# A build-time planner's order from backward schedules, repeated and replayed

## The chip, the cores and the metric

The kernel runs on one core of one Trainium2 chip. The metric is the device time in microseconds (us) of one execution. Times before are of three runs; the profile is of one more execution.

## The reference

One inference step of a one-layer hybrid decoder. A prompt of 2048 tokens and 8 decode sequences of 8 tokens go through the same layer:

```python
h = rmsnorm(x, norm_w)
z = h @ w_in                       # 1024 x 3600
q, k, v, qb, kb, vb, g_lr, gate_a, gate_b = split(z)
q, k = rope(rmsnorm(q)), rope(rmsnorm(k))
o_a = attend(q, k, v)              # 8 heads x 64; windows (128,1), (512,4), (2048,16), mixed by their softmax denominators
log_a = log_sigmoid(g_lr @ w_gate_up + b_gate) / 16
o_b, s_fin = gla_chunked(qb / 8, kb, vb, log_a, s0)   # 4 heads, key 64, value 128
o_b = rmsnorm(o_b, gla_norm_w)
mixed = concat(o_a * silu(gate_a), o_b * silu(gate_b))
y = x + mixed @ w_out
```

The decode tokens attend to caches of 2048 keys and values for each sequence and update a recurrent state. Outputs are `y` of both parts, the new keys and values, and the GLA states. All is float32 outside; the kernel splits float32 operands of the large products into two fp16 parts.

## The kernel before

The program is written as one long trace of instructions for five engines: PE (matmul), DVE, ACT, POOL and SP, which issues all the DMAs on its queue. It is tiled by 128 tokens, 16 tiles for the prompt.

Its stages, in the order of the code:

- Input projections (`project`, matmuls at L1614 into `acc_q`, `acc_k`, `acc_v`, `acc_qkb`, `acc_g`, `acc_vb`, `acc_gb`), each with its own block of weights, `load_w` at L1144 and L1145. Three weight blocks fit at a time. `post` evacuates them, to scratch tensors in DRAM (`vb_d`, `gw_d`, `ga_d` and others).
- Prompt attention (`attend`): scores `s` on PE (L894), mask and minimum on DVE (L902, which also writes to `o`), the exponential `p` on ACT (L905), transposes `t` on PE (L912), a split `pt` into fp16 halves on ACT, DVE or POOL (L874 to L879), products `O` on PE (L927).
- Decode-side dot products (`dot`, 128 of them): a product `pr` on POOL (L1469) and its sum `sck` on DVE (L1470). They share a region of SBUF with other things that the GLA stage opens later.
- GLA (`gla_core`, `gla_prompt`): small fp32 matmuls (`sc_e` at L730, `U` L1777, `O` L1785 and L1791), in a chain over 16 chunks through a state `Sbd`; `gla_out` scales the output (`ob_c`, L785) and stores it in `ob_d`. The gate-b projection `acc_gb` is woven with it.
- Output: `combine` loads three attention branches (`oc`), the GLA output and gates (`obl`, `gwl`, `gal`) and mixes them (`tc`, `mix`); the result is split into fp16 (`mt`), transposed (`tm`, L1950), copied (`mh`), and multiplied with the output weights (`Y`, L1985). Its buffers take the room of the GLA stage's buffers. `inv_o`, which every evacuation of `Y` needs, needs all of the gate-b projection.
- Decode attention (`sample_pair`), beside the output stage: value blocks of 1 MB (`sv_b`, L2265, 24 of them) and fp32 matmuls `OS` (L2234).

The order in which each engine runs its instructions isn't that of the code. At the end of the trace the class `Plan` reads all the instructions, works out which depends on which (`dep`) or must stay behind which (`behind`), prices each (`price`: `busy`, how long its engine is taken; `late`, when its result is there; `lands` for a DMA's landing), and runs a list scheduler over the whole program (`order`). That scheduler simulates the five engines and the DMA queue forwards in time; where an engine has several ready instructions it takes the one with the lowest `prio`. PE's true fp32 matmuls (`slow`) have a queue of their own, and `bias` makes it stay with the kind it is at. `fix` then writes the found order into the program as dependencies without semaphores, and the framework emits each engine's queue in that order.

Before, the priority came from one pass of `rank`: an instruction's longest path to the end of the program, with no regard to engines being taken by other work:

```python
plan = Plan(tc, nc)
far = plan.rank()
plan.fix(plan.order([-f for f in far], 2000.0)[1])
```

Of the kernel before, what the change touches and what calls it, by code (L numbers as in the profile page):

```python
# [7 lines left out]
F32 = mybir.dt.float32  # L8
# [43 lines left out]
class Plan:  # L52
# [3 lines left out]
    def __init__(self, tc, nc, cross=35.0, traffic=1.15, lanes=8, room=212832):  # L56

        self.tc, self.cross, self.traffic = tc, cross, traffic
        self.lanes, self.room = lanes, room
        traced = nc.cur_bb.bb.instructions  # L60
        self.at = {i.name: n for n, i in enumerate(traced)}
        self.ins = [
            i for i in traced
            if type(i).__name__ not in ("BassTilePoolBoundary", "InstTileManualSchedule")
        ]
        self.eng = [str(i.engine).split(".")[-1] for i in self.ins]
        self.bits, self.pools = {}, {p.id: p for p in tc.info.pools}
        self.read()
        self.depend()
        self.price()  # L70
# [192 lines left out]
    def price(self):  # L263
# [22 lines left out]
            return r * (2 if a.dtype in (F16, BF16) else 4)  # L286

        self.busy, self.late, self.lock = [], [], []
        self.slow, self.columns, self.lands = set(), {}, {}
        for i, e in zip(self.ins, self.eng):  # L290
            ts, os_ = tensors(i.ins), tensors(i.outs)
            kind = type(i).__name__
# [4 lines left out]
            elif e == "PE":  # L297
                n = cells(os_[0])
                size, place = tuple(i.tile_size)[1], tuple(i.tile_position or (0, 0))[1]
                wide = [x for x in range(4) if size == P or place <= 32 * x < place + size]  # L300
# [7 lines left out]
                else:  # L308
                    n *= 2 if step >= 4 else 1
                    busy, late = max(n / 2.4 + 2.4, 55.5), 165 + n / 2.4  # L310
                self.columns[len(self.busy)] = wide
                busy *= 1.03
                late = max(busy, late)
            elif e == "SP":
# [105 lines left out]

    def order(self, prio, bias=0.0):

        from heapq import heappop, heappush

        N = len(self.dep)
        left = [len(d) + len(b) for d, b in zip(self.dep, self.behind)]
        ready, start, done = [0.0] * N, [0.0] * N, [0.0] * N
        soon = {e: [] for e in self.ENGINES}
        now = {e: [] for e in self.ENGINES}
        wide = []  # L430
        free = {e: 0.0 for e in self.ENGINES}
        held = {"DVE": 0.0, "Pool": 0.0}
        column, last, mode, queue = [0.0] * 4, 0.0, False, 0.0
        out = {e: [] for e in self.ENGINES}
# [36 lines left out]
        def arrive(e, t):  # L471
            while soon[e] and soon[e][0][0] <= t:
                _, pr, n = heappop(soon[e])
                heappush(wide if e == "PE" and n in self.slow else now[e], (pr, n))

        for n in range(N):
            if not self.dep[n] and not self.behind[n]:
                released(n)
        for _ in range(self.real):
            best = None  # L480
            if len(out["SP"]) >= self.lanes:
                free["SP"] = max(free["SP"], done[out["SP"][-self.lanes]] + self.cross + 20)
# [12 lines left out]
            line = now[e]  # L495
            if e == "PE" and wide:
                if not line or wide[0][0] <= line[0][0] + (bias if mode else -bias):
                    line = wide
            _, n = heappop(line)
            out[e].append(n)  # L500
            start[n] = t
            if e == "SP":
                free[e] = t + self.busy[n]
                queue = max(queue, free[e]) + self.late[n]
                done[n] = queue + self.lands[n]
            elif e == "PE":
                at = self.columns[n]
                s = max(t, last + 6, max(column[c] for c in at))
                if (n in self.slow) != mode:
                    s, mode = max(s, max(column) + 93), not mode  # L510
                last = start[n] = s
                for c in at:
                    column[c] = s + self.busy[n]
                free[e] = max(s, min(column)) if len(at) < 4 else s + self.busy[n]
                done[n] = s + self.late[n] + (100 if mode else 0)
# [11 lines left out]
        return max(done), out  # L527

    def fix(self, out):

# [11 lines left out]
def tile_hymba(ctx: ExitStack, tc: tile.TileContext, A: dict):  # L542
# [1752 lines left out]
        weave(out, [sample_attention(), 4 * 9])  # L2295

    plan = Plan(tc, nc)
    far = plan.rank()
    plan.fix(plan.order([-f for f in far], 2000.0)[1])


# [92 lines left out]
```

## Time and profile before

| | |
|---|---|
| median of 3 runs | 1388.49 us (1387.33 to 1389.8) |
| the profiled execution's own time | 1387.66 us |
| its span, first to last instruction | 1385.1 us |
| mean granted TensorE clock | 0.97 |
| PE busy | 1244.2 us (90%) |
| DVE busy | 1008.1 us (73%) |
| ACT busy | 844.7 us (61%) |
| POOL busy | 639.5 us (46%) |
| DMA | 283.25 MB, 205 GB/s over the span |

Busy time is the time in which an engine had at least one instruction under way. PE's matmuls are pipelined, so a busy PE is not PE at its peak, and weight loads (PEld) run beside them. The granted clock is the share of full speed that TensorE's throttle gave; it is either 1 or 0.5 at a moment in this trace. The rest of the time lies in waits, which the prediction shows by stretch.

### The profile page before, as it was taken

How to read it: one execution, taken by the hardware profiler on the slowest of the kernel's cores; microseconds unless marked ns; L12 is line 12 of the kernel's file. 1: busy time of each engine (PE TensorE's matmuls, PEld its weight loads, DVE VectorE, ACT ScalarE, POOL GpSimd, SP SyncE). 2: the span in 40 equal slices, each digit the busy share in tenths (PEclk: the TensorE clock that was granted, in tenths of full speed). 3: DMA queues.
4: the chain of work that ended last, by engine and by line, in shares of the span. 5: the costliest groups of instructions: out<-in, count | busy, mean ns of one | idle time of the engine just before them, and what ended most of it. 6: DMA issues, size and time to landing. Idle time of an engine off the chain costs nothing.

```text
span 1385.1 us, 26375 instructions
## 1 busy us (share of the span) xinstructions
PE 1244.2 (90%) x8942; PEld 739.4 (53%) x8942; DVE 1008.1 (73%) x2459; ACT 844.7 (61%) x2259; POOL 639.5 (46%) x564
## 2 busy tenths in 40 slices
PE   5999988987889789998899999999989839999998
PEld 2444455555456556655667656665555415445443
DVE  6897787888889978767665338778889775566632
ACT  6465588786678869776778347787768541222220
POOL 0155447787677555543212546645574332233310
PEclk9999999998999999999999999999999969999999
DMA  8579747968986797899765534325334389999822
GB/s 298 179 194 268 206 132 202 226 199 213 207 288 178 170 308 242 248 249 280 187 181 154 144 102 110 109 84 179 103 100 145 104 309 344 343 380 345 323 79 70
DMA packets 236121, 283.25 MB, mean 205 GB/s; under 512 B 116353, under 2 KB 147154, under 8 KB 232914
## 3 DMA queue, kind: packets, MB, share of 16 engines
q1 hardware_dynamic: 235986, 281.57, 67.9%
q8 instruction: 70, 1.15, 0.4%
q14 instruction: 65, 0.53, 0.1%
HBM read 183.19 MB, written 75.24 MB: 187 GB/s over the span
## 4 chain that ended last, share of the span: by engine, by line
PE 36%; DVE 8%; ACT 7%; DMA 6%; issue 3%; POOL 1%; SPq 1%; DVEq 0%; ACTq 0%; POOLq 0%
PE Y L1985 10%; PE acc_vb L1614 4%; PE acc_g L1614 4%; PE acc_gb L1614 4%; DMA qb<-q_d 2%; PE OS L2234 1%; PE sc_e L730 1%; ACT p L905 1%; PE t L912 1%; PE O L1791 1%; PE acc_qkb L1614 1%; DMA o_d<-o 1%; DVE qbd L706 1%; PE O L1785 1%; PE O L927 1%
## 5 line engine op out<-in xcount | busy, mean ns | idle before, releaser
L1614 PEld LDWEIGHTS <-hr 128*128 128x128 f16 x1824 | 175.1, 99 | 125.0 <-issue 29.7
L1469 POOL TENSOR_TENSOR pr<-k,qb 128x512 f32<-128x512 f32 x128 | 176.9, 1382 | 133.4 <-DVE sck L1470 62.7
L905 ACT ACTIVATE p<-p,o 128x256 f32<-128x256 f32 (+1 forms) x384 | 172.7, 453 | 53.5 <-DVE o L902 43.7
L1614 PEld LDWEIGHTS <-hl 128*128 128x128 f16 x1248 | 119.7, 98 | 128.2 <-issue 18.7
L1985 PE MATMUL Y<-w_o,mh 128*128 128x512 f16 x768 | 181.1, 381 | 3.6 <-DVE xr L1992 1.7
L927 PE MATMUL O<-v,pt 128*128 128x128 f16 x1200 | 145.9, 224 | 8.6 <-POOL pt L879 3.5
L879 POOL TENSOR_TENSOR pt<-p,pt 128x512 f16<-128x512 f32 (+1 forms) x80 | 93.0, 1163 | 125.6 <-ACT pt L878 94.7
L912 PE MATMUL t<-ident,p 128*128 128x128 f32 x600 | 132.2, 294 | 16.3 <-ACT p L905 10.4
L1614 PE MATMUL acc_g<-w_g,hr 128*128 128x272 f16 (+1 forms) x768 | 130.6, 276 | 3.3 <-ACT vbs L1263 2.0
L1614 PE MATMUL acc_vb<-w_vb,hr 128*128 128x512 f16 x384 | 122.1, 384 | 1.6 <-DVE so_g L1163 1.5
L927 PEld LDWEIGHTS <-pt 128*128 128x128 f16 x1200 | 100.2, 101 | 43.3 <-POOL pt L879 7.2
L1470 DVE TENSOR_REDUCE sck<-pr 128x8 f32<-128x512 f32 x128 | 87.3, 682 | 48.9 <-POOL pr L1469 48.2
L1614 PE MATMUL acc_v<-w_v,hl 128*128 128x512 f16 x384 | 120.2, 384 | 2.0 <-DMA hl<-ht 1.0
L1614 PE MATMUL acc_k<-w_k,hl 128*128 128x512 f16 x384 | 114.8, 379 | 4.5 <-DVE vp L1276 2.9
L1614 PE MATMUL acc_q<-w_q,hl 128*128 128x512 f16 x384 | 116.2, 379 | 2.8 <-ACT zs_q L1189 2.4
L1985 PEld LDWEIGHTS <-mh 128*128 128x128 f16 x768 | 71.2, 98 | 84.5 <-issue 7.5
L894 PE MATMUL s<-kk,qq 128*128 128x256 f16 (+1 forms) x512 | 84.8, 270 | 29.4 <-DVE o L902 21.7
L912 PEld LDWEIGHTS t<-ident,p 128*128 128x128 f32 x600 | 79.3, 147 | 50.1 <-ACT p L905 28.0
L1614 PE MATMUL acc_gb<-w_gb,hr 128*128 128x512 f16 x384 | 95.7, 399 | 7.8 <-DVE so_gb L1163 7.8
L902 DVE CUSTOM_DVE_ANT_0 p<-s,m3w,scl_s 128x128 f32<-128x128 f32 (+1 forms) x256 | 87.8, 396 | 19.8 <-DMA o_d<-o 8.9
L2033 POOL TENSOR_TENSOR tc<-oc,w 128x512 f32<-128x512 f32 x32 | 42.8, 1354 | 118.7 <-DVE w L2025 67.9
L1614 PE MATMUL acc_qkb<-w_qkb,hr 128*128 128x512 f16 x288 | 85.1, 379 | 0.0
(534 smaller groups left out, 2723.1 us busy)
## 6 DMA issues: line engine op xcount, KB each, us to landing
k<-in_cache_k_win SPq DMA_DIRECT2D x104, 256.0 KB
sv_b<-in_cache_v_win SPq DMA_DIRECT2D x24, 1024.0 KB
hr<-h_d SPq DMA_DIRECT2D x44, 512.0 KB
qb<-q_d SPq DMA_DIRECT2D x64, 256.0 KB
oc<-o_d SPq DMA_DIRECT2D x48, 264.0 KB
o_d<-o SPq DMA_DIRECT2D x64, 132.0 KB
x<-in_x_prompt SPq DMA_DIRECT2D x16, 512.0 KB
h_d<-hl SPq DMA_DIRECT2D x16, 512.0 KB
```

The source lines that it names most:

```text
L706: DVE.tensor_tensor(qbd[:, :, :n].rearrange("p i (m B) -> p i m B", B=B), qv[:, :, 1, :].unsqueeze(1).to_broadcast([P, 2, M, B]), ev[:, 1: ...
L879: POOL.tensor_tensor(l, f, h, ALU.subtract)
L894: PE.matmul(s_ps[:, i * w : (i + 1) * w], q, k, start=(n == 0), stop=(n == len(prods) - 1),)
L902: DVE.tensor_tensor_reduce(s[:, sl], s_ps[:, sl], mask, neg, BIG, ALU.add, ALU.min, nmf(i))
L905: ACT.activation(s[:, sl], s[:, sl], AF.Exp, bias=nmf(i), scale=-1.0, accum_out=denf(i))
L912: PE.transpose(p_ps[:, i * P : (i + 1) * P], t["s"][:, i * P : (i + 1) * P], ident[:])
L927: PE.matmul(o_, t["pt"][:, c, (i * nb + b) * P : (i * nb + b + 1) * P], vf(i, b), start=(n == 0), stop=(n == 2 * nb - 1),)
L1469: POOL.tensor_tensor(pr[:], kt, qt, ALU.mult)
L1470: DVE.tensor_reduce(out, pr[:].rearrange("p (u k d) -> p u k d", u=2, k=4), AX.X, ALU.add)
L1614: PE.matmul(z, a_[:, k, :], w[:, p_, k, cols], start=(k == 0 and i == 0), stop=(k == KT - 1 and i == 2),)
L1985: PE.matmul(Y[:], a_[:, k, :], w_[:, part, k, :512], start=(i == 0), stop=(i == len(prods) - 1),)
L2033: eng.tensor_tensor(t_[:], oc[:, g, :, 0:64], w[:, g].unsqueeze(2).to_broadcast([P, NH, HD]), ALU.mult,)
```

## The change

No operation of the computation changes; what changes is the order in which the planner puts them.

- `settle` replaces the single pass. It runs eight rounds of: schedule forwards with `order`, then backwards from the end with `backward`, and take the places of the backward schedule as the next round's priorities. The first round uses `rank` as before.
- While it plans, it uses other prices: every DMA lands 500 ns later, SP's transfers take 1.1 times as long, a hand-over between engines costs 50 ns in place of 35. The bias is 1000 in place of 2000.
- Each round's order is replayed (`replay`, the engines' order held) in four disturbed versions of the true prices (`other`: DMA times drawn at random, a quarter of the other instructions 30 ns longer). The order with the lowest sum of the four ends is kept.
- `order` has a model of the TensorE clock: array work (`area`) in a window of 3413 ns. Where it was under 0.4 of the window, PE's instructions of the next window cost twice as much. And PE holds on to fp32 matmuls by the bias only while the recent array work is over half a window (`keep`); else fp32 must be ahead of fp16 by the bias.

```diff
+        self.window, self.least = 3413.0, 0.5
...
+                four = 4 if len(self.busy) in self.slow else 2 if ts[0].dtype == F32 else 1
+                rows = -(-list(ts[0].ap)[0][1] // 32) / 4
+                self.area[len(self.busy)] = four * cells(os_[0]) / 2.4 * rows * len(wide) / 4
...
             if e == "PE" and wide:
-                if not line or wide[0][0] <= line[0][0] + (bias if mode else -bias):
+                while recent and recent[0][0] < t - self.window:
+                    active -= recent.popleft()[1]
+                keep = mode and active > self.least * self.window
+                if not line or wide[0][0] <= line[0][0] + (bias if keep else -bias):
                     line = wide
...
+                if int(s // self.window) > turn:
+                    half = work < 0.4 * self.window or int(s // self.window) > turn + 1
+                    turn, work = int(s // self.window), 0.0
+                work += self.area[n]
+                active += self.area[n]
+                recent.append((s, self.area[n]))
+                own = self.busy[n] * (2 if half else 1)
                 for c in at:
-                    column[c] = s + self.busy[n]
+                    column[c] = s + own
...
+    def backward(self, prio):
...
+        for n in [n for n in range(N) if not left[n]]:
+            ready[n] = self.late[n]
+            if self.eng[n] == "SP":
+                ready[n] += self.busy[n] + self.lands[n]
+            released(n)
+        for _ in range(self.real):
+            best = None
+            for e in self.ENGINES:
+                while soon[e] and soon[e][0][0] <= free[e]:
+                    heappush(now[e], heappop(soon[e])[1:])
+                t = free[e] if now[e] else soon[e][0][0] if soon[e] else None
+                if t is not None and (best is None or t < best[0]):
+                    best = t, e
...
+            _, n = heappop(now[e])
+            place[n] = free[e] = t + self.busy[n]
...
+    def other(self, seed):
...
+        for n in range(self.real):
+            if self.eng[n] == "SP":
+                q.late[n] *= 0.4 + 0.6 * r.expovariate(1)
+                q.lands[n] += 400 * (r.expovariate(1) - 0.5)
+            elif self.eng[n] != "PE":
+                more = r.choice((0, 0, 0, 30))
+                q.late[n] += more
+                q.busy[n] += more
+        return q
...
+    def settle(self, rounds, land, traffic, cross, bias, others=4):
+
+        true = Plan.__new__(Plan)
+        true.__dict__.update(self.__dict__)
+        self.rank()
+        true.nxt, true.then = self.nxt, self.then
+        others = [true.other(k) for k in range(others)]
+        self.lands = {n: x + land for n, x in self.lands.items()}
+        self.late = [
+            x * (traffic if self.eng[n] == "SP" else 1.0) for n, x in enumerate(self.late)
+        ]
+        self.cross = cross
+        prio, best = [-f for f in self.rank()], None
+        for _ in range(rounds):
+            out = self.order(prio, bias)[1]
+            prio = [-x for x in self.backward(self.start)]
+            end = sum(o.replay(out) for o in others)
+            if best is None or end < best[0]:
+                best = end, out
+        return best[1]
...
-    far = plan.rank()
-    plan.fix(plan.order([-f for f in far], 2000.0)[1])
+    plan.fix(plan.settle(8, 500.0, 1.1, 50.0, 1000.0))
```

More of the change, by code (lines that the diff above doesn't have):

```diff
@@ L288, in price @@
         self.busy, self.late, self.lock = [], [], []
-        self.slow, self.columns, self.lands = set(), {}, {}
+        self.slow, self.columns, self.lands, self.area = set(), {}, {}, {}
         for i, e in zip(self.ins, self.eng):
@@ L421, in order @@
     def order(self, prio, bias=0.0):
+        from collections import deque
         from heapq import heappop, heappush
@@ L433, in order @@
         column, last, mode, queue = [0.0] * 4, 0.0, False, 0.0
+        turn, work, half, recent = 0, 0.0, True, deque()
+        active = 0.0
         out = {e: [] for e in self.ENGINES}
@@ L511, in order @@
                 last = start[n] = s
+                if int(s // self.window) > turn:
[5 more added lines that the diff above has]
+                own = self.busy[n] * (2 if half else 1)
                 for c in at:
-                    column[c] = s + self.busy[n]
-                free[e] = max(s, min(column)) if len(at) < 4 else s + self.busy[n]
-                done[n] = s + self.late[n] + (100 if mode else 0)
+                    column[c] = s + own
+                free[e] = max(s, min(column)) if len(at) < 4 else s + own
+                done[n] = s + self.late[n] + (100 if mode else 0) + own - self.busy[n]
             else:
@@ L527, in order, with after @@
         return max(done), out
+    def after(self, n, x):
+        e, o, late = self.eng[n], self.eng[x], self.late[n]
+        if e == "gate" or (o == e == "PE"):
+            return 0.0
+        if e == "SP":
+            late += self.busy[n] + self.lands[n]
+        elif n in self.slow:
+            late += 100
+        if o == "gate":
+            return late
+        if o == e:
+            return late + (self.cross if e == "SP" else -60.0)
+        return late + self.cross + (20 if o == "PE" else 0)
@@ new lines, in backward, with released, before @@
+    def backward(self, prio):
+        from heapq import heappop, heappush
+        N = len(self.dep)
+        left = [len(d) + len(b) for d, b in zip(self.nxt, self.then)]
+        place, ready = [0.0] * N, [0.0] * N
+        soon = {e: [] for e in self.ENGINES}
+        now = {e: [] for e in self.ENGINES}
+        free = {e: 0.0 for e in self.ENGINES}
+        def released(n):
+            line = [n]
+            while line:
+                n = line.pop()
+                if self.eng[n] == "gate":
+                    place[n] = ready[n]
+                    line += before(n)
+                else:
+                    heappush(soon[self.eng[n]], (ready[n] - self.busy[n], -prio[n], n))
+        def before(n):
+            free_now = []
+            for x in self.dep[n]:
+                ready[x] = max(ready[x], place[n] + self.after(x, n))
+                left[x] -= 1
+                if not left[x]:
+                    free_now.append(x)
+            for x in self.behind[n]:
+                ready[x] = max(ready[x], place[n])
+                left[x] -= 1
+                if not left[x]:
+                    free_now.append(x)
+            return free_now
+        for n in [n for n in range(N) if not left[n]]:
[11 more added lines that the diff above has]
+                    best = t, e
+            t, e = best
+            while soon[e] and soon[e][0][0] <= t:
+                heappush(now[e], heappop(soon[e])[1:])
+            _, n = heappop(now[e])
+            place[n] = free[e] = t + self.busy[n]
+            if e == "PE" and len(self.columns[n]) < 4:
+                free[e] = t + max(6.0, self.busy[n] * len(self.columns[n]) / 4)
+            for x in before(n):
+                released(x)
+        return place
@@ new lines, in other @@
+    def other(self, seed):
+        import random
+        r, q = random.Random(seed), Plan.__new__(Plan)
+        q.__dict__.update(self.__dict__)
+        q.late, q.busy, q.lands = list(self.late), list(self.busy), dict(self.lands)
+        for n in range(self.real):
[7 more added lines that the diff above has]
+        return q
@@ new lines, in replay @@
+    def replay(self, out):
+        q = Plan.__new__(Plan)
+        q.__dict__.update(self.__dict__)
+        q.then, q.behind = [list(x) for x in self.then], [set(x) for x in self.behind]
+        for order in out.values():
+            for a, b in zip(order, order[1:]):
+                if a not in q.behind[b]:
+                    q.behind[b].add(a)
+                    q.then[a].append(b)
+        return q.order([0.0] * len(self.dep), 0.0)[0]
+    def settle(self, rounds, land, traffic, cross, bias, others=4):
[17 more added lines that the diff above has]
+        return best[1]
```

## The prediction

> **What bounds the kernel now.** I read the top of the page first, then busy time by stage, then who PE waited for in the two stages where it stands, then the chain through the deepest hole. The page's head, and of its chain of work the shares by engine:
>
> ```profile
> span 1385.1 us, 26375 instructions
> ## 1 busy us (share of the span) xinstructions
> PE 1244.2 (90%) x8942; PEld 739.4 (53%) x8942; DVE 1008.1 (73%) x2459; ACT 844.7 (61%) x2259; POOL 639.5 (46%) x564
> ...
> PE 36%; DVE 8%; ACT 7%; DMA 6%; issue 3%; POOL 1%; SPq 1%; DVEq 0%; ACTq 0%; POOLq 0%
> ```
>
> PE is the busiest engine and the largest part of the chain. It stands 1385.1 - 1244.2 = 140.9 us. An order can only win from that idle time and from work that ran at a low clock; PE's instructions stay. The table of stretches says where they lie (after the length: PE, weight loads, DVE, ACT, POOL, each busy us and count, then granted clock, DMA share, GB/s):
>
> ```profile
> core 0: us, PE busy (x) PEld busy (x) DVE busy (x) ACT busy (x) POOL busy (x), PEclk, DMA share, GB/s
> 0.00:35.00 35.00, 19.10 (x98) 9.81 (x99) 23.30 (x55) 22.11 (x38) 0.39 (x6) 1.00 0.89 299
> 35.00:173.00 138.00, 131.44 (x630) 59.93 (x629) 112.24 (x225) 74.00 (x150) 56.83 (x49) 1.00 0.73 212
> 173.00:520.00 347.00, 294.74 (x2179) 193.09 (x2179) 298.95 (x750) 262.31 (x764) 229.90 (x174) 0.97 0.81 212
> 520.00:692.00 172.00, 157.97 (x1251) 105.36 (x1250) 123.93 (x399) 133.12 (x418) 78.46 (x62) 0.98 0.89 242
> 692.00:831.00 139.00, 137.14 (x1030) 91.34 (x1028) 66.82 (x232) 83.64 (x270) 47.83 (x54) 1.00 0.51 145
> 831.00:1108.00 277.00, 258.69 (x2033) 160.41 (x2032) 225.44 (x452) 201.22 (x511) 154.46 (x166) 0.95 0.38 117
> 1108.00:1142.50 34.50, 11.83 (x64) 6.21 (x63) 27.71 (x71) 14.37 (x27) 13.45 (x12) 0.65 0.89 308
> 1142.50:1350.00 207.50, 204.80 (x1532) 100.50 (x1531) 121.77 (x270) 51.50 (x81) 58.17 (x44) 1.00 0.81 302
> 1350.00:1385.10 35.10, 28.50 (x140) 12.72 (x138) 7.97 (x12) 2.49 (x4) 0.00 (x0) 1.00 0.21 74
> ```
>
> Subtracting PE from each length: 15.9 us idle while the first loads come, 6.6 in the first projections, 52.3 in 173 to 520 (attention woven with projections; DVE 298.95 of 347, 86%, is nearly as full as PE's 85%), 14.0 and 1.9 in the next two, 18.3 in the GLA stage, 22.7 in the hand-over hole of 34.5 us, 2.7 and 6.6 in the output stage. The output stage is full of PE work, so an order has nothing to win there.
>
> **The change part by part.** The same 26,375 instructions are issued; planning is done while the program is built. So nothing is added or removed on an engine, and every term is idle time that goes or comes. The profiled execution took 1387.66 us, 2.6 more than its span; the median of the runs, 1388.49, is 0.8 more. Terms are worked against 1387.66.
>
> *Backward priorities at the hand-over.* The old priority of an instruction is its longest path to the end, as if every engine were free. The new one, from the second round on, is its place in a backward schedule in which each engine does one thing at a time; PE's 233.3 us of output work (204.80 + 28.50) therefore weigh on whatever must come before them. The chain through the hole, from the chain of work in order of time (start, length, what), then PE's one wait, then what PE did just before (from the timeline), then where the gate-b projection lay:
>
> ```profile
> 1111.50 1.15 ACT ob_c L785 x4
> ...
> 1113.52 0.45 SPq L2002
> ...
> 1115.47 5.09 DMA gwl<-gw_d
> 1120.59 4.55 DMA gal<-ga_d
> ...
> 1134.74 1.06 ACT mt L1940
> ...
> 1139.16 0.61 PE Y L1985
> ```
>
> ```profile
> PE tm L1950 <- ACT mt L1940: 19.3, 1, 19.3
> ```
>
> ```profile
> 1102.84 0.61 PE L1791 MATMUL O<-vb,full 128*128 128x128 f32 x4
> 1103.29 10.31 PE L1614 MATMUL acc_gb<-w_gb,hr 128*128 128x512 f16 x47
> ```
>
> ```profile
> 831.00:1108.00 277.00, 90.07 (x359) 10.45 (x14) 0.95 0.38 117
> 1108.00:1142.50 34.50, 5.59 (x26) 1.49 (x2) 0.65 0.89 308
> ```
>
> The last GLA output leaves PE at 1103.45, its scaling (`ob_c`) comes 8 us later, then the loads of `combine` (queued on SP behind the store of `ob_c`), `mix`, `mt`, and only at 1139.16 the first `Y`. PE has 10.31 us of gate-b matmuls behind the last GLA output and then nothing. 90.07 of the 95.66 us of gate-b work had been spent before 1108. If the plan runs the GLA chain ahead of it and keeps more of it back, the hole is covered by work that exists. Ends: 0, since the GLA chain leans on DVE (225 of 277 us busy there) and may not come earlier; and all of it, 22.7 plus half of the 5.43 us that ran at half clock (row further down), 25. I take the middle, 12: the cover exists, but only as much as GLA can be advanced. If that cover goes somewhere else, the hole grows by the same 10.3.
>
> *Backward priorities in the attention stage.* What PE waits for there, and the decode-side dot products `pr`/`sck` by stretch (DVE, then POOL):
>
> ```profile
> PE s L894 <- DVE o L902: 20.0, 21, 2.8
> ```
>
> ```profile
> 173.00:520.00 347.00, 59.31 (x87) 123.47 (x88) 0.97 0.81 212
> 520.00:692.00 172.00, 28.02 (x41) 53.44 (x41) 0.98 0.89 242
> ```
>
> PE's largest wait is for DVE's mask-and-minimum, and 59.31 of DVE's 298.95 us are dot products that no PE work of this stage needs. They must be done before the GLA pools take their memory, and 520 to 692 leaves DVE 48 us free. Ends: 0, and the rate of the next stretch, where the same attention has PE busy 157.97 of 172 (91.8%): 294.74 / 0.918 = 321, so 26 won. I take 13, half, because DVE's share limits what can be moved, not only the order. Behind a late dot product on POOL stands the subtraction `pt` that feeds `O`; both gain or lose together.
>
> *The clock and the bias.* The planner now doubles PE's prices after a stretch of 3413 ns with under 0.4 of array work, and stays with fp32 matmuls by the bias (2000, now 1000) only while array work is above one half; else it prefers fp16. The granted clock in the GLA stage, one case with the stretch before it, then the sum of the five half-clock stretches of that stage (937.6, 971.7, 1009.3, 1043.4, 1081.0), and the hole:
>
> ```profile
> 934.20:937.60 3.40, 2.43 (x31) 1.43 (x28) 3.32 (x10) 3.12 (x10) 0.00 (x0) 1.00 0.81 247
> 937.60:941.00 3.40, 3.40 (x14) 1.33 (x12) 3.40 (x6) 0.08 (x1) 1.62 (x2) 0.50 0.94 304
> ```
>
> ```profile
> sum 27.20, PE 23.89 PEld 11.25 DVE 25.87 ACT 15.57 POOL 6.17; mean PE 4.78 PEld 2.25 DVE 5.17 ACT 3.11 POOL 1.23
> ```
>
> ```profile
> 1118.50:1142.40 23.90, 5.43 (x33) 3.23 (x34) 21.61 (x52) 9.15 (x15) 9.91 (x7) 0.50 1.02 361
> ```
>
> 23.89 us of PE work ran at half clock, so 12 us are lost. Ends: 0 and 12; I take 6, since fp16 filler can be put between the fp32 groups in some of these places only. In sentences apart: the Trainium skill, "TensorE: Matmul & The Clock Gate", section "HAM oscillation — how this bites in real kernels", gives the rule as no PE gaps over about 3.4 us. By that rule no such gap lies before 937.6, the clock term is 0, and the sum would be 6 us worse. The row above differs: PE was busy 2.43 of 3.40 us and the next stretch got 0.50.
>
> The lower bias can make more changes between fp32 and fp16. No row prices a change by itself; the nearest is the wait of fp32 weight loads for nothing that shows:
>
> ```profile
> PEld sc_e L730 <- issue: 14.6, 28, 2.3
> ```
>
> That is 0.52 us each, at most; twice as many would cost 14.6, none 0. The loads lie beside other matmuls, so I take 2 lost, near the lower end.
>
> *Margins.* Each transfer is planned 500 ns later and 1.1 times as long, each hand-over between engines 50 instead of 35 ns. Loads are asked for earlier in an order that SP keeps strictly: what SP is made to wait for holds the loads behind it. Bounds: gain, the 15.9 us of the start at most, which stand on the first loads themselves, so 0; loss, a share of the output stage, where the 24 loads of 1 MB run from 1130.5 to 1283.8 and leave 101 us to the end:
>
> ```profile
> L2265 SPq DMA_DIRECT2D sv_b<-in_cache_v_win x24: 327/333/892, 1130.5 to 1283.8; - x24
> ```
>
> That slack hides tens of us of shift; I take 0. Choosing among eight rounds by replays with other DMA times gives no time of its own; it makes an order that lives from one exact arrival less likely.
>
> Sum: -12 - 13 - 6 + 2 = -29. 1387.66 - 29 = 1358.7, and against the median 1359.5.
>
> **The rivals.** (1) *The dots crowd the attention.* The backward pass sees the dots ahead of both GLA and the long output stage and may pull the remaining 41 into 173 to 520. POOL has room (117 us idle, 41 dots are 53.44), so it can. DVE would go from 298.95 to 327 us; at the 86% at which PE began to wait, the stretch becomes 327 / 0.861 = 380, so +33. The stretch after it, 92% full on PE, returns little. With the hand-over, clock and bias terms (-16) the net is +17: 1405. It decides for slower once half of them (16 of 33) have moved. Against it: the planner counts DVE's time in both directions.
>
> (2) *Same time.* The replays choose an order that differs in places but keeps the hole, whose chain is latency, and DVE's limit in attention; or the first round wins, which still has the old kind of priority. Then 1388.5. For it: PE is 90% busy. Against it: 47 matmuls were there to hold back, and the limit of DVE is not one in 520 to 692.
>
> (3) *The clock doesn't follow.* The half-clock stretches stay because the GLA chain itself has too little work for the array; the 6 us of that term fall out: 1365.5. The skill's rule named above would give this case too. Against it stands the row at 934.2, where what came before was fp32 work that could have been mixed.
>
> **How the numbers follow.** The forecast as summed, 0.52; rival 3, 0.13; rival 2, 0.09; rival 1, 0.26. A change of 0.2% (2.8 us) is about what a measurement of this kernel can tell from none. So faster 0.65, same 0.09, slower 0.26. The predicted time is 1359.5. The lowest is all best ends: 25 + 26 + 12 = 63 off 1388.5, 1326. The highest is rival 1, 1405. The forecast's own range, with the two largest terms between a quarter and all of their ends, is 1326 to 1376.
>
> **What would show it.** Hand-over: the wait of `tm` for `mt`, now 19.3, under 10, and gate-b matmuls within 25 us of the first `Y`. Attention: PE idle by stretch down from 52 to about 39 with fewer dots inside, and `s` waiting less for `o`. Clock: the mean above 0.97, fewer 0.50 stretches beside `sc_e`. Margins: no new PE wait for a load in the output stage. The prediction is wrong if DVE's busy time in the attention stretch rises, if a hole opens between attention and GLA, where PE has only 1.9 us idle now, or if value loads end near the end of the span.

## The result, and the profile after

The changed kernel takes 1337.01 us (median of 4 runs, 1335.32 to 1341.44) against 1389.14 (4 runs, 1387.33 to 1396.17) for the kernel before: a ratio of 0.9621, 95% interval 0.9579 to 0.9662, so 3.4 to 4.2% faster. Predicted were 1359.5 us and faster. The direction held; the size was 52 us where 29 were forecast. The profiled execution took 1335.32 us.

The order that was kept is that of the second round, the first with backward priorities; the six rounds after it did no better in the replays. An experiment with two rounds therefore differs from the changed kernel by its own edit alone. The traces agree: the run of two rounds with the last gate-b work held back (below) has the same order of matmuls as the changed kernel up to the 7078th of 8942. The changed kernel's lines stand 141 lines lower than those of the kernel before (L1614 is now L1755).

The head of the page after the change, and the shares of its chain of work by engine:

```profile
span 1333.5 us, 26352 instructions
## 1 busy us (share of the span) xinstructions
PE 1233.1 (92%) x8942; PEld 731.4 (55%) x8942; DVE 1014.5 (76%) x2459; ACT 839.6 (63%) x2259; POOL 642.3 (48%) x564
...
PE 42%; ACT 10%; DMA 9%; DVE 9%; issue 5%; POOL 4%; SPq 1%; DVEq 0%; POOLq 0%; ACTq 0%
```

PE issues the same 8942 matmuls, and the other engines as many instructions as before; the 23 fewer in the head are among those that the page doesn't count as busy. PE stands 1333.5 - 1233.1 = 100.4 us instead of 140.9 (-40.5), and is busy 1233.1 instead of 1244.2 (-11.1). Together that is the whole 51.6 us of the span. The table of stretches, columns as in the prediction, says where:

```profile
0.00:35.00 35.00, 19.78 (x101) 10.20 (x102) 25.93 (x58) 22.42 (x38) 0.39 (x6) 1.00 0.87 297
35.00:173.00 138.00, 130.53 (x627) 59.72 (x625) 114.27 (x220) 74.56 (x152) 56.06 (x50) 0.99 0.77 216
173.00:520.00 347.00, 325.09 (x2480) 210.89 (x2480) 306.22 (x797) 288.28 (x847) 211.59 (x157) 1.00 0.80 211
520.00:692.00 172.00, 155.76 (x1299) 108.40 (x1298) 131.04 (x441) 129.59 (x435) 89.01 (x69) 0.98 0.96 261
692.00:831.00 139.00, 135.50 (x1009) 87.34 (x1006) 81.14 (x197) 78.97 (x234) 77.90 (x86) 0.99 0.55 151
831.00:1108.00 277.00, 246.62 (x1854) 147.17 (x1854) 233.98 (x496) 193.78 (x479) 154.53 (x158) 0.93 0.48 159
1108.00:1142.50 34.50, 34.50 (x360) 19.34 (x358) 14.57 (x42) 7.17 (x16) 6.28 (x6) 1.00 0.96 361
1142.50:1333.50 191.00, 185.33 (x1223) 88.31 (x1220) 107.38 (x215) 44.87 (x63) 46.58 (x34) 1.00 0.69 248
```

Lengths minus PE, against the prediction's table: the attention stretch 173 to 520 went from 52.3 us idle to 21.9 (-30.4); GLA stage and hand-over hole together from 41.0 to 30.4 (831 to 1108 now holds both, and the start of the output); the output stage from 9.3 to 5.7 (-3.6); the first two stretches and the two after attention gave back 4.0. PE did 2480 matmuls in the attention stretch where it did 2179, at a granted clock of 1.00.

PE's waits over the whole span, two rows (engine, tile and line, what it waited for: total us, times, longest), and then, by stretch, the dot products `pr` and `sck` (DVE, then POOL):

```profile
PE tm L2091 <- ACT mt L2081: 18.6, 1, 18.6
...
PE s L1035 <- DVE o L1043: 7.9, 15, 1.7
```

```profile
173.00:520.00 347.00, 44.75 (x66) 94.39 (x67) 1.00 0.80 211
520.00:692.00 172.00, 34.12 (x50) 66.44 (x49) 0.98 0.96 261
```

PE's largest wait of before, for DVE's mask-and-minimum, fell from 20.0 to 7.7 us in the attention stretch (over the whole span, as in the row, from 22.4 to 7.9). The dots inside the attention stretch went from 87 to 66, so DVE has 14.6 us less of them there; it is still busier than before (306.22 against 298.95), since 21.8 us of other work came in. The wait in the hole hardly moved. From the timeline of PE (start, length, what, idle before it), then busy time in the two parts of the hole (columns as above), then the chain of work:

```profile
1051.55 9.88 PE L1755 MATMUL acc_gb<-w_gb,hr 128*128 128x512 f16 x45
...
1081.91 1.03 PE L2091 MATMUL tm<-ident,mt 128*128 128x128 f16 x8 [18.60 <-ACT mt L2081]
...
1084.06 1.89 PE L2126 MATMUL Y<-w_o,mh 128*128 128x512 f16 x4 [1.11 <-ACT mh L2092]
```

```profile
1051.55:1061.43 9.88, 9.88 (x49) 4.55 (x47) 6.91 (x21) 5.63 (x14) 5.36 (x6) 1.00 0.49 153
1061.43:1084.06 22.63, 2.75 (x17) 1.50 (x16) 20.85 (x48) 9.62 (x18) 9.82 (x8) 0.59 0.91 320
```

```profile
1058.27 1.15 ACT ob_c L926 x4
...
1061.83 4.33 DMA gw_d<-gw
...
1073.53 3.11 POOL tc L2174 x2
...
1078.27 1.26 POOL tc L2180
```

The hole is the one of before, 55 us earlier: 45 gate-b matmuls behind the last GLA output instead of 47, and then 22.63 - 2.75 = 19.9 us of nothing. From `ob_c` to the first `Y` it took 27.7 us (1111.50 to 1139.16) and now 25.8 (1058.27 to 1084.06). DVE is full in it: busy 20.85 of 22.63 us, of which 6.86 go to eight splits of output weights (`w_o`, L1286); between the last gate-b matmul and the first `Y` of before it spent 6.40 us on them. The low clock lasts longer than before: 11.54 us of PE's work around the hole ran at half clock (1065.6 to 1096.3, so 12 us into the output stage), 5.43 before.

Four tiles show how early each stage lies (shortest, median and longest duration in ns, then first and last start in us). Before:

```profile
L1469 POOL TENSOR_TENSOR pr<-k,qb x128: 1260/1272/2260, 203.8 to 676.2; 128x512 f32<-128x512 f32 x128
L730 PE MATMUL sc_e<-qbd,ks x768: 218/222/369, 828.6 to 1084.8; 128*64 128x64 f32 x192
L927 PE MATMUL O<-v,pt x1200: 216/219/315, 172.7 to 755.9; 128*128 128x128 f16 x172
L1614 PE MATMUL acc_vb<-w_vb,hr x384: 376/379/634, 671.2 to 933.4; 128*128 128x512 f16 x192
```

After:

```profile
L1610 POOL TENSOR_TENSOR pr<-k,qb x128: 1260/1273/3673, 208.3 to 731.7; 128x512 f32<-128x512 f32 x128
L871 PE MATMUL sc_e<-qbd,ks x768: 219/222/368, 804.0 to 1035.4; 128*64 128x64 f32 x192
L1068 PE MATMUL O<-v,pt x1200: 216/219/231, 172.6 to 724.1; 128*128 128x128 f16 x172
L1755 PE MATMUL acc_vb<-w_vb,hr x384: 376/379/634, 616.4 to 887.3; 128*128 128x512 f16 x192
```

The last dot comes 55 us later, attention ends 32 us earlier, GLA starts 25 us earlier, and the `vb` projection is done 46 us earlier. From the first `sc_e` to the last GLA `O` it took 274.6 us before and takes 247.4 now: 27 more are won. Three more come in the hole, and the output stage takes 3 back: 52.

### The profile page after: what moved, and what is told of

It reads as the page before. It is cut to its first block, busy times and chain, and to the rows that moved or that the text cites. A ratio compares the mean times of both kernels' runs of the same rounds, so it can differ in the third digit from the quotient of the medians.

```text
span 1333.5 us, 26352 instructions
## 1 busy us (share of the span) xinstructions
PE 1233.1 (92%) x8942; PEld 731.4 (55%) x8942; DVE 1014.5 (76%) x2459; ACT 839.6 (63%) x2259; POOL 642.3 (48%) x564
## 4 chain that ended last, share of the span: by engine, by line
PE 42%; ACT 10%; DMA 9%; DVE 9%; issue 5%; POOL 4%; SPq 1%; DVEq 0%; POOLq 0%; ACTq 0%
PE Y L2126 12%; PE acc_gb L1755 4%; PE acc_vb L1755 3%; PE acc_g L1755 3%; ACT p L1046 3%; PE OS L2375 2%; PE acc_qkb L1755 2%; POOL pr L1610 2%; PE sc_e L871 2%; DMA o_d<-o 2%; DMA qb<-q_d 1%; PE t L1053 1%; DVE p L1043 1%; DMA ga_d<-so_g 1%; PE s L1035 1%
## 5 line engine op out<-in xcount | busy, mean ns | idle before, releaser
L1755 PEld LDWEIGHTS <-hr 128*128 128x128 f16 x1824 | 173.5, 99 | 124.3 <-issue 24.8
L1755 PEld LDWEIGHTS <-hl 128*128 128x128 f16 x1248 | 119.8, 98 | 127.4 <-issue 13.6
L2126 PE MATMUL Y<-w_o,mh 128*128 128x512 f16 x768 | 185.0, 386 | 3.2 <-ACT mh L2092 2.2
L1068 PE MATMUL O<-v,pt 128*128 128x128 f16 x1200 | 134.4, 220 | 8.1 <-POOL pt L1020 3.4
L1053 PE MATMUL t<-ident,p 128*128 128x128 f32 x600 | 127.2, 283 | 7.1 <-ACT p L1046 2.8
L1755 PE MATMUL acc_g<-w_g,hr 128*128 128x272 f16 (+1 forms) x768 | 119.7, 279 | 5.8 <-ACT vbs L1404 4.4
L1755 PE MATMUL acc_vb<-w_vb,hr 128*128 128x512 f16 x384 | 113.5, 384 | 8.3 <-DVE so_g L1304 8.0
L1755 PE MATMUL acc_v<-w_v,hl 128*128 128x512 f16 x384 | 118.5, 384 | 0.2 <-DMA hl<-ht 0.2
L1068 PEld LDWEIGHTS <-pt 128*128 128x128 f16 x1200 | 93.2, 98 | 40.1 <-POOL pt L1020 8.5
L1611 DVE TENSOR_REDUCE sck<-pr 128x8 f32<-128x512 f32 x128 | 87.1, 680 | 34.9 <-POOL pr L1610 34.6
L1755 PE MATMUL acc_q<-w_q,hl 128*128 128x512 f16 x384 | 107.3, 382 | 5.0 <-ACT zs_k L1330 5.0
L1755 PE MATMUL acc_k<-w_k,hl 128*128 128x512 f16 x384 | 106.8, 379 | 1.3 <-DVE vp L1417 1.0
L1755 PE MATMUL acc_gb<-w_gb,hr 128*128 128x512 f16 x384 | 92.2, 383 | 1.6 <-ACT vbs L1404 1.2
L1053 PEld LDWEIGHTS t<-ident,p 128*128 128x128 f32 x600 | 73.8, 141 | 35.1 <-ACT p L1046 20.7
L2092 ACT ACTIVATE mh<-tm 128x1024 f16<-128x1024 f16 x32 | 32.3, 1021 | 92.2 <-PE tm L2091 82.1
```

The lines of the kernel that those rows point to most:

```text
L1053: PE.transpose(p_ps[:, i * P : (i + 1) * P], t["s"][:, i * P : (i + 1) * P], ident[:])
L1068: PE.matmul(o_, t["pt"][:, c, (i * nb + b) * P : (i * nb + b + 1) * P], vf(i, b), start=(n == 0), stop=(n == 2 * nb - 1),)
L1611: DVE.tensor_reduce(out, pr[:].rearrange("p (u k d) -> p u k d", u=2, k=4), AX.X, ALU.add)
L1755: PE.matmul(z, a_[:, k, :], w[:, p_, k, cols], start=(k == 0 and i == 0), stop=(k == KT - 1 and i == 2),)
L2092: ACT.activation(mhl[:, a], pt[:], AF.Copy)
L2126: PE.matmul(Y[:], a_[:, k, :], w_[:, part, k, :512], start=(i == 0), stop=(i == len(prods) - 1),)
```

## The experiments

**Which half of the change: priorities or prices.** First the changed planner stopped after its first round: new prices, bias and clock model, but the old priorities (longest path).

```diff
-    plan.fix(plan.settle(8, 500.0, 1.1, 50.0, 1000.0))
+    plan.fix(plan.settle(1, 500.0, 1.1, 50.0, 1000.0))
```

> One round only: the old priorities (longest path), with the new margins, the bias of 1000 and the clock model; no backward schedule. If the backward priorities carry the gain: 1375 to 1392 us, PE idle between 173 and 520 us near 50 as before, first Y near 1139. If the margins, bias and clock carry it: 1335 to 1350, PE idle there near 22.

1370.32 us, ratio 0.9872 (0.9855 to 0.9889): between the two ranges expected. Then the opposite: one backward pass, with the old prices and bias and without the clock model.

```diff
-                keep = mode and active > self.least * self.window
+                keep = mode
...
-                own = self.busy[n] * (2 if half else 1)
+                own = self.busy[n]
...
-            if best is None or end < best[0]:
+            if True:
...
-    plan.fix(plan.settle(8, 500.0, 1.1, 50.0, 1000.0))
+    plan.fix(plan.settle(2, 0.0, 1.0, 35.0, 2000.0))
```

> One backward schedule for the priorities and nothing else new: the old prices (no added landing, hand-over of 35 ns), bias 2000, no clock model. If the backward priorities carry the gain: 1335 to 1355. If margins and clock are needed to make the order hold on the chip: 1370 or more, with new waits of PE for DMAs.

1359.88 us, ratio 0.9798 (0.978 to 0.9815): again between the two. The page of the first, then of the second:

```profile
span 1367.3 us, 26412 instructions
...
PE 1252.8 (92%) x8942; PEld 737.2 (54%) x8942; DVE 1017.9 (74%) x2459; ACT 844.7 (62%) x2259; POOL 633.5 (46%) x564
```

```profile
span 1356.7 us, 26371 instructions
...
PE 1233.0 (91%) x8942; PEld 735.3 (54%) x8942; DVE 1011.7 (75%) x2459; ACT 843.2 (62%) x2259; POOL 637.8 (47%) x564
```

So both halves win, 1.3% and 2.0%, and 0.9872 x 0.9798 = 0.967 is nearly the whole (0.9621). The prices, the bias and the clock model under old priorities take 26 us from PE's idle time and make PE 8.6 us busier. The backward priorities without any clock model take 17 us of idle time and all of the 11.2 us of busy time (1233.0, the changed kernel 1233.1). The fall of PE's busy time thus comes without the planner's knowledge of the clock. In the attention stretch, 173 to 520, PE is idle 34.9 us in the first run and 27.1 in the second, 52.3 before.

**The clock model and the bias.** All as changed with one backward pass, but neither doubled prices nor the rule on recent array work:

```diff
-                keep = mode and active > self.least * self.window
+                keep = mode
...
-                own = self.busy[n] * (2 if half else 1)
+                own = self.busy[n]
...
-            if best is None or end < best[0]:
+            if True:
...
-    plan.fix(plan.settle(8, 500.0, 1.1, 50.0, 1000.0))
+    plan.fix(plan.settle(2, 500.0, 1.1, 50.0, 1000.0))
```

> The changed kernel with one backward schedule, without the clock model and without the rule on fp32 work; margins and bias as changed. If the clock term of the prediction holds: 6 to 12 us slower than the changed kernel, 1343 to 1349, with more half-clock stretches in the GLA stage. If it was worth nothing: within 4 us of 1337.

1352.02 us, ratio 0.9735 (0.9705 to 0.9765).

```profile
span 1351.4 us, 26353 instructions
...
PE 1233.7 (91%) x8942; PEld 733.3 (54%) x8942; DVE 1021.3 (76%) x2459; ACT 842.0 (62%) x2259; POOL 634.4 (47%) x564
```

Doubled prices and rule together are worth 15 us between the medians, more than the 6 to 12 expected, and almost none of it in PE's busy time (1233.7 against 1233.1): PE is idle 117.7 us against 100.4. More half clock in the GLA stage was expected, and there is none: its stretches sum to 10.20 us in both kernels. Of the 18 us between the spans, 13 are lost before the first `sc_e` (817 against 804). Next only the rule taken out, the doubled prices kept; then, with both in, the old bias.

```diff
-                keep = mode and active > self.least * self.window
+                keep = mode
...
-            if best is None or end < best[0]:
+            if True:
...
-    plan.fix(plan.settle(8, 500.0, 1.1, 50.0, 1000.0))
+    plan.fix(plan.settle(2, 500.0, 1.1, 50.0, 1000.0))
```

> The changed kernel with one backward schedule, with the doubled prices after low array work, but staying with fp32 by the bias always, as before (the rule on recent array work out). If the rule, by mixing fp16 into fp32 stretches, won the clock term: 1345 to 1354. If the doubled prices did: within 4 us of 1337.

1341.77 us, ratio 0.968 (0.9651 to 0.9709). By the medians the rule is worth 5 us, which isn't resolved: the intervals of this run and of the changed kernel overlap, and the time lies between the two ranges expected. The doubled prices carry about 10 of the 15 us, with intervals that just touch (0.9709 and 0.9705).

```diff
-            if best is None or end < best[0]:
+            if True:
...
-    plan.fix(plan.settle(8, 500.0, 1.1, 50.0, 1000.0))
+    plan.fix(plan.settle(2, 500.0, 1.1, 50.0, 2000.0))
```

> The changed kernel with one backward schedule and the bias at 2000 as before, clock model, fp32 rule and margins as changed. If the bias is part of what the clock changes won: 1342 to 1352. If it is the clock model and the rule: within 4 us of 1337.

1346.04 us, ratio 0.9712 (0.9685 to 0.9738), apart from the changed kernel's interval: the lower bias wins 9 us between the medians, as the first branch expected. In the profiled executions PE is busy 1228.9 us of 1340.9 there: 4.2 less than in the changed kernel, and idle 112.0 us instead of 100.4.

**The margins.** One backward pass at the true prices of DMAs and hand-overs:

```diff
-            if best is None or end < best[0]:
+            if True:
...
-    plan.fix(plan.settle(8, 500.0, 1.1, 50.0, 1000.0))
+    plan.fix(plan.settle(2, 0.0, 1.0, 35.0, 1000.0))
```

> The changed kernel with one backward schedule, clock model and bias of 1000, without the margins (landing, transfer time and hand-over at the old prices). If margins only shift the plan: 1335 to 1345. If they keep loads from coming late: 1355 or more, and PE, DVE or POOL wait more for DMAs.

1341.27 us, ratio 0.966 (0.9643 to 0.9677). 4 us between the medians, and the intervals overlap: the margins only shift the plan.

**The dots.** Is it enough that they come later? In the kernel before, the dots and their loads were made 90 us less urgent, then 45 us:

```diff
+    for n in plan.dots():
+        far[n] -= 90000.0
     plan.fix(plan.order([-f for f in far], 2000.0)[1])
```

> The kernel before, old priorities, prices, bias, no clock model; only the instructions of the decode-side dot products (their loads too) get a priority 90 us less urgent. If deferring the dots out of the attention stage is what the backward priorities won: 1350 to 1368, the last acc_k near 415 us (447 before). If the gain is spread over all priorities and the dots are a by-product: 1378 to 1392.

1388.14 us, ratio 1.0017 (0.9996 to 1.0038), in the second range.

> As the kernel before with late dot products, but deferred by 45 us of priority, not 90. There the attention ended earlier and the gain was lost again before the GLA stage, whose start waited for the last dots. If that was the reason: last dots near 735 us, GLA's first sc_e below 815, 1365 to 1375. If deferring the dots wins nothing by itself: 1380 to 1392.

1382.83 us, ratio 0.997 (0.9946 to 0.9993), in the second range too. Tile rows of the first, then of the second:

```profile
L1477 POOL TENSOR_TENSOR pr<-k,qb x128: 1252/1272/2242, 205.7 to 789.0; 128x512 f32<-128x512 f32 x128
L738 PE MATMUL sc_e<-qbd,ks x768: 219/222/368, 822.7 to 1086.3; 128*64 128x64 f32 x192
L935 PE MATMUL O<-v,pt x1200: 216/219/314, 173.4 to 737.4; 128*128 128x128 f16 x172
```

```profile
L1477 POOL TENSOR_TENSOR pr<-k,qb x128: 1261/1272/2260, 205.4 to 748.8; 128x512 f32<-128x512 f32 x128
L738 PE MATMUL sc_e<-qbd,ks x768: 219/222/369, 830.0 to 1086.0; 128*64 128x64 f32 x192
L935 PE MATMUL O<-v,pt x1200: 216/219/314, 173.7 to 756.9; 128*128 128x128 f16 x172
```

With 90 us attention ended at 737 instead of 756 and the `qkb` projection at 616 instead of 639, but GLA started at 823 all the same, 34 us after the last dot at 789. With 45 us the last dot lay near that of the changed kernel (749, 732), and attention ended at 757: it was no earlier than before. Inside the attention stretch the late dots did win; the stretches of the run with 90 us show where it went:

```profile
173.00:520.00 347.00, 314.21 (x2387) 207.42 (x2387) 290.99 (x770) 283.66 (x830) 189.88 (x145) 0.98 0.74 192
520.00:692.00 172.00, 155.30 (x1228) 102.33 (x1225) 128.95 (x416) 126.90 (x411) 79.50 (x64) 0.98 0.94 251
692.00:831.00 139.00, 132.11 (x949) 86.27 (x947) 79.03 (x206) 75.90 (x233) 81.56 (x86) 1.00 0.71 198
831.00:1108.00 277.00, 248.73 (x1924) 153.36 (x1924) 227.56 (x440) 194.39 (x489) 156.05 (x162) 0.93 0.35 110
```

PE is idle 32.8 us in the first of them, 19.5 less than before, and 2.7, 5.0 and 10.0 more in the next three; it also worked longer at half clock in the GLA stage (mean clock 0.93, before 0.95). This run's chain of work passes the last dots (`pr` at 786.93), gate work and a load (`bm<-in_c_bm`, 3.71 us) on its way to the first decode-side GLA output (`O_s`) at 804.3, which started at 782 before. Now the other way, the dots 90 us more urgent in the second round of the changed planner:

```diff
+            for n in self.dots():
+                prio[n] -= 90000.0
-            if best is None or end < best[0]:
+            if True:
...
-    plan.fix(plan.settle(8, 500.0, 1.1, 50.0, 1000.0))
+    plan.fix(plan.settle(2, 500.0, 1.1, 50.0, 1000.0))
```

> The changed kernel with one backward schedule; only the dot products' instructions get a priority 90 us more urgent in the second round, which puts them where they were before. If the dots carry the backward gain: 1358 to 1372, like the kernel of the first round alone, the last acc_k near 435. If not: within 8 us of 1337.

1358.28 us, ratio 0.9791 (0.9758 to 0.9823), at the edge of the first range: 21 us of the 52 are gone. Its dots, and its attention stretch:

```profile
L1620 POOL TENSOR_TENSOR pr<-k,qb x128: 1258/1277/2257, 208.6 to 658.0; 128x512 f32<-128x512 f32 x128
```

```profile
173.00:520.00 347.00, 307.32 (x2248) 199.57 (x2247) 300.60 (x764) 266.47 (x782) 231.21 (x174) 0.95 0.84 215
```

PE is idle 39.7 us there instead of 21.9. The last dot lies 18 us ahead even of the kernel before (658, 676). So late dots are needed for 21 of the 52 us; 31 are left without them, and by themselves they bring next to nothing.

**The hole.** As changed with one backward pass, everything on the gate-b accumulators of the last four tiles 20 us less urgent, so that more of them are left for the hole:

```diff
+            for n in self.gate_b():
+                prio[n] += 20000.0
-            if best is None or end < best[0]:
+            if True:
...
-    plan.fix(plan.settle(8, 500.0, 1.1, 50.0, 1000.0))
+    plan.fix(plan.settle(2, 500.0, 1.1, 50.0, 1000.0))
```

> The changed kernel with one backward schedule, and in the second round all that belongs to the gate-b accumulators of the last four prompt tiles gets a priority 20 us less urgent. If the hole before the first Y is open because gate-b work was spent too early, as the prediction had it: PE's wait of tm for mt below 12 us and 1325 to 1333. If the hole is the latency of the chain from the last GLA output to Y, with all cover already used: the wait stays at 16 to 20 us and the time within 4 us of 1337.

1332.75 us, ratio 0.9591 (0.9565 to 0.9618); the interval overlaps the changed kernel's. The time fits the first branch and the wait the second, so neither is confirmed. Its PE timeline in the hole:

```profile
1052.43 11.40 PE L1765 MATMUL acc_gb<-w_gb,hr 128*128 128x512 f16 x52
1063.67 0.38 PE L2311 MATMUL R<-ident,Scg 128*128 128x128 f32 x2
1080.13 1.04 PE L2101 MATMUL tm<-ident,mt 128*128 128x128 f16 x8 [16.09 <-ACT mt L2091]
```

52 matmuls stand behind the last GLA output instead of 45, and the wait went from 18.6 to 16.1 us. The first `Y` came at 1082 instead of 1084. 20 us of urgency put only seven more matmuls into the hole, which stays as long as the chain from the GLA output to `mt`. That chain got 2.3 us shorter here (30.4 us from the last GLA output to the first `Y`, 32.7 in the changed kernel). Most splits of `w_o` moved up under the gate-b matmuls: between the last of these and the first `Y` DVE spends 1.90 us on them instead of 6.86. Whether that is the reason wasn't tested by itself.

**The choice by replays.** The order of the fourth round, and one of the fifth round under other margins that had the best replays of several hundred orders:

```diff
-            if best is None or end < best[0]:
+            if True:
...
-    plan.fix(plan.settle(8, 500.0, 1.1, 50.0, 1000.0))
+    plan.fix(plan.settle(4, 500.0, 1.1, 50.0, 1000.0))
```

> The changed kernel with the order of the fourth round, whatever the replays say; the kernel as changed keeps the second round, the first that uses a backward schedule. If the choice by replays tells good rounds from worse ones: 1341 to 1350. If rounds after the first backward one are all alike on the chip: 1333 to 1341. If repeating is what improves: below 1333.

1338.66 us, ratio 0.9647 (0.961 to 0.9684), in the range for rounds that are all alike.

```diff
-            if best is None or end < best[0]:
+            if True:
...
-    plan.fix(plan.settle(8, 500.0, 1.1, 50.0, 1000.0))
+    plan.fix(plan.settle(5, 400.0, 1.05, 55.0, 1000.0))
```

> The changed kernel with other margins (landing 400 ns, transfers 1.05 times, hand-over 55 ns) and the order of the fifth round, picked from some four hundred orders by replays with six other disturbed versions. If replays rank orders this finely: 1325 to 1333. If the last per cent is chance of the draws: 1334 to 1346.

1333.85 us (6 runs), ratio 0.9595 (0.9565 to 0.9625), between the two ranges. Once the backward priorities are in, orders of different rounds can't be told apart here, and what the replays rank among them is below what these runs resolve. The larger step is from the first round (1370.32) to the second, 33 of the 52 us.

Where each kernel's stages lie, first or last starts in us of its profiled execution, with PE's idle time and matmuls in the attention stretch, 173 to 520:

| | last dot | attention `O` last | `sc_e` first | `acc_vb` last | GLA `O` last | first `Y` | span | PE idle, 173 to 520 | matmuls there |
|---|---|---|---|---|---|---|---|---|---|
| before | 676 | 756 | 829 | 933 | 1103 | 1139 | 1385 | 52.3 | 2179 |
| dots 90 us later | 789 | 737 | 823 | 932 | 1104 | 1140 | 1387 | 32.8 | 2387 |
| dots 45 us later | 749 | 757 | 830 | 935 | 1104 | 1140 | 1386 | 38.6 | 2299 |
| first round | 674 | 743 | 821 | 906 | 1080 | 1115 | 1367 | 34.9 | 2262 |
| backward alone | 740 | 730 | 811 | 918 | 1079 | 1112 | 1357 | 27.1 | 2426 |
| dots early | 658 | 739 | 824 | 908 | 1074 | 1107 | 1357 | 39.7 | 2248 |
| no clock model | 743 | 738 | 817 | 901 | 1070 | 1103 | 1351 | 23.1 | 2423 |
| after | 732 | 724 | 804 | 887 | 1051 | 1084 | 1334 | 21.9 | 2480 |

From the first `Y` on all of them need 245 to 253 us. The gain is made before it, and in every kernel that wins, the projections (`acc_vb`) are ahead of where they were, by 15 to 46 us.

## Why the prediction was right, and where its steps failed

The direction held, and the size came within a factor of two partly by luck. Of the 29 us forecast, the 12 of the hand-over came to about 3; the attention stretch gave twice its 13; and 27 us came in the GLA stage, for which the sum had only the clock's 6. (The range's lower end, 1326, takes the clock at its best end too, and not the two largest terms alone.)

*Hand-over, -12: wrong step.* The prediction took the cover of the hole to be a matter of what is kept back. The wait of `tm` fell from 19.3 to 18.6, not under 10; from the start of the last GLA outputs to the first `Y` it won about 3 us, and PE's work at half clock around it rose from 5.43 to 11.54 us. In place of missing cover stands a chain from the GLA output to `mt`, and DVE, on which much of it runs, is full: 20.85 of 22.63 us. In the chain of after, the store of the gates (`gw_d<-gw`, 4.33 us) stands inside it, and the gates come from gate-b; that gate-b work can't be put off much since the output needs it is argued from this, not shown. In the run with gate-b held, seven more matmuls left a wait of 16.1 us. How much of the hole is latency, and how much DVE's other work in it, such as the splits of `w_o`, stays open.

*Attention, -13: right place, too small.* It won 30.4 us in 173 to 520 and gave 2.2 back in the next stretch, past the upper end of 26. The step that failed is the half, taken because "DVE's share limits what can be moved": DVE's share went from 86% to 88%, while PE's went from 85% to 93.7% (325.09 of 347). The cap was too low as well, by 2 us: the rate of the stretch 520 to 692 (91.8%) was taken as the best that attention allows. The mechanism named was a part of it. Fewer dots and the smaller wait for `o` came as forecast, and taking back the late dots cost 21 us. Late dots with the old priorities won up to 19.5 us of idle time in this stretch as well, but lost it again in the next three and came to 0.3% or nothing. What the backward priorities add is that attention, projections and dots are moved against each other together, and that the gain is kept: the two stretches after attention gave back 3.8 us. Which pair of priorities does it stays open.

*The sign named for failure fired without a failure.* DVE's busy time in the attention stretch rose by 7.3 us, which the prediction gave as a proof of being wrong. It was a bad sign: DVE's total can rise because the stage itself goes faster. The time of the dots inside the stretch, 59.31 to 44.75, was the one to name, and it refutes rival 1. Another sign held without saying much: the last gate-b matmul lies 22.6 us ahead of the first `Y`, under the 25 named, and lay 25.6 ahead of it before.

*Clock, -6: right size in the GLA stage, with more than one cause.* The half-clock stretches of the GLA stage, as sums (length, PE, PEld, DVE, ACT, POOL, then means): in the changed kernel (from 939.3, 6.8 us, and from 1028.1, 3.4 us), in the first round alone (from 912.5 and 960.3), and with backward priorities alone (four of 3.4 us, from 862.1, 957.6, 1022.5 and 1053.2):

```profile
sum 10.20, PE 9.60 PEld 6.65 DVE 9.77 ACT 7.05 POOL 5.16; mean PE 4.80 PEld 3.32 DVE 4.88 ACT 3.52 POOL 2.58
```

```profile
sum 13.80, PE 9.61 PEld 6.25 DVE 10.85 ACT 10.46 POOL 5.75; mean PE 4.80 PEld 3.13 DVE 5.42 ACT 5.23 POOL 2.88
```

```profile
sum 13.60, PE 13.29 PEld 8.84 DVE 11.62 ACT 9.05 POOL 9.08; mean PE 3.32 PEld 2.21 DVE 2.90 ACT 2.26 POOL 2.27
```

23.89 us of PE work at half clock became 9.60: 7.1 us won where 6 were forecast, so rival 3 fell. The prediction put this down to the planner's clock model and the bias. Under the old priorities these, with the margins, leave 9.61 us, and backward priorities without them leave 13.29: either half brings most of the term, and the runs don't say which one does it in the whole. The first round alone paid for it elsewhere: 41 us of the attention stretch ran at half clock, 24 before. In the whole span PE's busy time is 11.1 less; backward priorities alone gave the same 1233.0 us. Busy time isn't a measure of the clock alone: the first round did as much PE work at half clock as the kernel before (56 us over the span) and was busy 8.6 us longer. The doubled prices and the rule do win 15 us, but in idle time, which no term of the sum had. How doubled prices in a plan come to save waits is open.

*Bias, +2: wrong sign.* The old bias costs 9 us more. The cost that the prediction named may be there: PE is busy 4.2 us less with the old bias, and its order changes 202 times between true fp32 matmuls (those that aren't transposes) and others, the changed kernel's 236 times, the kernel before 196. But runs with a bias of 1000 and other rounds or rules differ as much in PE's busy time (1229.1 in the fourth round, 1236.7 without the rule), so this isn't resolved. What the term left out is that the order changes with the bias: PE's idle time is 11.6 us larger with the old one.

*Margins, 0: held* within the 0.4% that separate the medians, not separable from none.

*The GLA stage: no term.* 27 us came between the first `sc_e` and the last GLA `O`, of which the prediction priced the clock alone. The projections that are woven there had been pulled ahead by 46 us (`acc_vb` last at 887 against 933), so less of them was left: between those two points PE's time in `acc_vb` and `acc_g` fell from 83.5 to 60.6 us. As a whole PE is busy 17.6 us less there (256.54, now 238.92) and idle 9.5 us less (18.3, now 8.8). Moved work alone isn't enough: with the dots 90 us later only 65.6 us of these projections lay there, and the stage took 281 us, 28.3 of them idle and 41 at half clock. No run tested it by itself.

*What a measurement can tell.* The prediction called 0.2% resolvable. 17 runs of the kernel before on one chip went from 1380.1 to 1394.75 us, 1.1%; the intervals above, of 4 to 10 runs, are 0.2 to 0.4% wide on either side.

## What to carry to other kernels

A longest-path priority doesn't see that engines are taken; if the busiest engine idles in a stage where another is nearly as full, try priorities from a backward schedule with one thing at a time on each engine before tuning constants, and expect the first such pass to bring most of the gain (here 33 of 52 us between the first round and the second). Deferring the work that seems in the way may only move the idle time to later stages: look at when the next stage starts, not at how much earlier the present one ends. Before covering a hole between stages, look at the chain through it and at the engine that is full in it; here seven more matmuls of cover went with 2.5 us off a wait of 18.6.

## What the runs showed of the hardware

PE can be busy for most of a stretch and still get half the clock in the next. Two stretches of the run with gate-b held:

```profile
994.60:998.00 3.40, 3.03 (x39) 1.99 (x39) 3.01 (x7) 2.92 (x8) 3.40 (x4) 1.00 0.61 204
998.00:1001.40 3.40, 3.32 (x9) 1.34 (x9) 2.99 (x13) 3.30 (x11) 0.57 (x1) 0.50 0.01 5
```

PE was busy 3.03 of 3.40 us, among others with `sc_e` matmuls of 128x64 in fp32, and the clock was then 0.50. The Trainium skill, "TensorE: Matmul & The Clock Gate", section "HAM oscillation — how this bites in real kernels", warns of PE gaps over about 3.4 us; there is none here, as there was none in the prediction's row at 934.2. In both cases the work ahead was mostly small fp32 matmuls, so how much of the array they use may be the measure; no run varied that alone. And planning with a clock model doesn't by itself give more clock: summed over the span's half-clock stretches, the first-round order had 86 us of them, the kernel before 82, the changed kernel 53.
